# The T1 operands' norm, difference and split go tile by tile and ahead of the fourth product

## The chip, the cores and the metric

The kernel runs on one core of a Trainium2 chip. The metric is the device time of one execution in microseconds. Beside the runs there is one execution taken by the hardware profiler; its rows give times from the first instruction on. TensorE's instructions stand under PE (matmul) and PEld (weight load), VectorE's under DVE, ScalarE's under ACT, GpSimd's under POOL, and the queue that issues most transfers under SP.

## The reference

One encoder layer for two sequences of 512 tokens (s0, the prompt, and s1, the sample), width 1024, in float32. What matters here are its last two parts:

```
h = h + concat(y_pool, y_att) @ w_o
u2 = rms_norm(h, ln2)
h = h + (silu(u2 @ w_gate) * (u2 @ w_up)) @ w_down        # 1024 -> 2816 -> 1024
gate = sigmoid(rms_norm(h, ple_norm) @ w_ple_gate)        # 1024 -> 1024
return h + gate * (p @ w_ple_proj)
```

`rms_norm` divides each token's row by its root mean square and multiplies by a gain per feature.

## The kernel before, in words

Activations lie with features on the 128 partitions and the 512 tokens of a sequence along the free dimension; a feature tile is 128x512. Every float32 product is made of three matmuls (`mm3`, L155 to L157): each operand is split into a high part (ScalarE, L128) and a low part, the rest (VectorE or GpSimd, L131), and high x high (L155), high x low of the activations (L156) and low x high (L157) are summed in PSUM.

Gate, up, down and the embeddings' gate are multiplied in the Winograd form of Strassen's scheme: the two sequences and the two halves of the features make a 2x2 block matrix of activations, two 128-wide column blocks of a weight and the two halves of its rows make the other, and seven products take the place of eight. The activations' operands are B11 and B21 (the first and the second half of s0's normed features) and B22 (the second half of s1's), as they are, and T1 = x12 - x11, T2 = x22 - T1, T4 = x21 - T2, T3 = x22 - x12, where x11 and x21 are s0's halves and x12 and x22 are s1's. Each operand is four tiles of 128 features, so each product is 4 x 3 = 12 matmuls.

`seven` (L679) is a generator that issues the seven products of one pair of weight columns: B11 into a bank a, B21 into a bank c, then it yields; then T1 into b, T2 on top of a, T4 into d, T3 on top of a, B22 on top of b. `got` (L711) copies a, b, and d out of PSUM on ScalarE (L714, into a buffer of the tag F) and adds on DVE (L717). `values4` and its callers make the outputs of them. Weights come from `stationary` (L629): a raw load of 512 KB (tag R, two buffers, L141, SP queue), totals of weight blocks on DVE (L641, tag G, four buffers), splits into eight buffers of tag W; `fill` asks for the next one whenever a product has taken one.

Four pairs are started ahead: their first two products need only s0, and while they run, DVE prepares what s1 gives. `normed_first` (L737) makes B11 and B21, `normed_rest` (L745) the five other operands. A norm is one DVE instruction a tile (`normed`, L727), which reads h, the gain and rb, a PSUM bank of tag g that holds 1/rms for all partitions; rb is made by `norm_rows`. Banks of c, b and d come alternately from the tags pt and g, two banks each; the fourth a is in the tag y. `difference` (L624, instruction L626) makes T1 in an F buffer and T3 in a G buffer; T2 (L756) and T4 (L759) are written over T1.

The order of instructions on an engine isn't the order of the program text: a planner simulates the program and gives each engine, whenever it is free, the earliest instruction of the text that is ready then and has its buffer. The order is fixed at build time; on the chip an engine waits for semaphores. In gate/up (L876 on) a pair is one f for `w_gate` or `w_up`, products of gate and up are multiplied and their seven operands are stored to HBM for the down stage (`spill`, L842), which loads them through the POOL queue (L917). At the embeddings' gate (L971 on) there are four pairs in all, which are started together and finished in order; their outputs go to HBM through the SP queue (L968).

Of the kernel before, what the change touches and what calls it, by code (L numbers as in the profile page):

```python
# [82 lines left out]
G_LN1, G_LN2, G_PLE, G_QA, G_KVA, G_PS, G_QN, G_KN, G_END = 0, 8, 16, 24, 27, 29, 33, 34, 35  # L83
# [3 lines left out]
def hybrid_layer(ctx: ExitStack, tc: tile.TileContext, a: dict, out: bass.AP):  # L87
# [10 lines left out]
    def sbuf(s, tag, shape, dt):  # L98
        return pool.tile([P] + shape, dt, tag=tag, name=nm(s), bufs=BUFS[tag])

    def At(s, tag="A", dt=F32R):
        return sbuf(s, tag, [2, T], dt)
# [9 lines left out]
    def eng(name, i=0):  # L112

        return nc.gpsimd if TURNS[name][i % len(TURNS[name])] == "p" else nc.vector

    def Ps(s, tag=None):
        if tag is None:
            tag = ALL_BANKS[turn[0] * 3 % 8]
            turn[0] += 1
        return psum.tile([P, T], F32, tag=tag, name=nm(s), bufs=PSUM_BUFS[tag])  # L120
# [4 lines left out]
    def split(hi, lo, src, hi_eng="act", lo_eng=nc.vector):  # L125

        if hi_eng == "act":
            nc.scalar.activation(hi, src, AF.Copy)  # L128
        else:
            nc.vector.tensor_copy(hi, src)  # L130
        lo_eng.tensor_tensor(lo, src, hi.bitcast(F32), op=ALU.subtract)  # L131
# [21 lines left out]
    def mm3(ps, lhs, rhs, first, last, more=False):  # L153

        nc.tensor.matmul(ps, lhs[0], rhs[0], start=first, stop=False, skip_group_check=more)  # L155
        nc.tensor.matmul(ps, lhs[0], rhs[1], start=False, stop=False, skip_group_check=more)  # L156
        nc.tensor.matmul(ps, lhs[1], rhs[0], start=False, stop=last, skip_group_check=more)  # L157

    def act(t, sl=slice(0, T), rows=P):
        return t[:rows, 0, sl], t[:rows, 1, sl]  # L160
# [27 lines left out]
    def norm_columns(sq):  # L188

        ps = Ps("st", "g")  # L190
        for t in range(NT):
            nc.tensor.matmul(ps[:, t:t + 1], sq[:, tok(t)], ones[:, 0:1], start=True, stop=True)
        base = col("base")
        nc.vector.tensor_scalar(base[:, :NT], ps[:, :NT], 1.0 / D, EPS, op0=ALU.mult, op1=ALU.add)
        return rsqrt(base[:, :NT], NT, "r")

    def norm_rows(r, copy=True):

        diag = Ft("diag")
        for t in range(NT):  # L200
            nc.vector.tensor_scalar(diag[:, tok(t)], ident, r[:, t:t + 1], None, op0=ALU.mult)
        ps = Ps("rb", "g")
        nc.tensor.matmul(ps, ones, diag, start=True, stop=True)
        if not copy:
            return ps
        rb = Ft("rb")
        nc.scalar.activation(rb, ps, AF.Copy)
        return rb
# [410 lines left out]
    def pieces(u, name, src, tag, lo):  # L619
        d = At("u", tag)  # L620
        split(d[:, 0, :], d[:, 1, :], src, lo_eng=lo)
        u.setdefault(name, []).append(d)

    def difference(x, y, e, tag="F"):  # L624
        d = sbuf("td", tag, [T], F32)
        e.tensor_tensor(d, x, y, op=ALU.subtract)  # L626
        return d
# [44 lines left out]
    def fill():  # L672
        while len(made) < AHEAD:
            w = next(stream, None)
            if w is None:
                return
            made.append(w)

    def seven(u, n, got, a_tag=None, tags=(None,)):  # L679


        def product(ps, b, first):
            w = made.pop(0)
            for j in range(n):
                mm3(ps, (w[:, 0, j * P:(j + 1) * P], w[:, 1, j * P:(j + 1) * P]), act(b[j]), first and j == 0, j == n - 1,
                    not first)
            fill()
            return ps

        def bank(name):  # L690
            t = tags[turn[0] % len(tags)]
            if t is not None:
                turn[0] += 1
            return Ps(name, t)

        a = product(Ps("a", a_tag), u["B11"], True)
        got(0, a)
        got(1, product(bank("c"), u["B21"], True))
        yield
        b = product(bank("b"), u["T1"], True)  # L700
        got(2, b)
        got(3, product(a, u["T2"], False))
        got(4, product(bank("d"), u["T4"], True))
        got(5, product(a, u["T3"], False))
        got(6, product(b, u["B22"], False))
# [19 lines left out]
    def normed(q, gc, k, rb, dst, i):  # L725
        if eng("norm", i) is nc.vector:
            nc.vector.scalar_tensor_tensor(dst, q.h[k], gcol(gc + k), rb[0], op0=ALU.mult, op1=ALU.mult)  # L727
        else:
            nc.scalar.activation(dst, q.h[k], AF.Copy, scale=gcol(gc + k))
            if len(rb) == 1:  # L730
                rb.append(Ft("rb"))
                nc.scalar.activation(rb[1], rb[0], AF.Copy)
            nc.gpsimd.tensor_tensor(dst, dst, rb[1], op=ALU.mult)

    HALF = KD // 2
# [7 lines left out]
                pieces(u, name, s0.u[j][:, i, :], TAGS[name], eng(f"n{i}", j))  # L743

    def normed_rest(gc, u, rb):  # L745
        x = [At("x1", "A", F32) for _ in range(HALF)]
        x12, x22 = ([v[:, i, :] for v in x] for i in range(2))
        for j in range(HALF):
            normed(s1, gc, j, rb, x12[j], 2)
        t = []  # L750
        for j in range(HALF):
            t.append(difference(x12[j], s0.u[j][:, 0, :], eng("tdif", 0)))
            pieces(u, "T1", t[j], TAGS["T1"], eng("n2", j))
        for j in range(HALF):
            normed(s1, gc, j + HALF, rb, x22[j], 3)
            eng("tdif", 1).tensor_tensor(t[j], x22[j], t[j], op=ALU.subtract)  # L756
            pieces(u, "T2", t[j], TAGS["T2"], eng("n3", j))
        for j in range(HALF):
            eng("tdif", 2).tensor_tensor(t[j], s0.u[j][:, 1, :], t[j], op=ALU.subtract)  # L759
            pieces(u, "T4", t[j], TAGS["T4"], eng("n6", j))  # L760
        t3 = []
        for j in range(HALF):
            t3.append(difference(x22[j], x12[j], eng("t3", j), "G"))
            pieces(u, "B22", x22[j], TAGS["B22"], eng("n4", j))
        for j in range(HALF):
            pieces(u, "T3", t3[j], TAGS["T3"], eng("n5", j))

    def run(*gens):
        for g in gens:
            for _ in g:  # L770
                pass
# [46 lines left out]
    u = {}  # L818
# [4 lines left out]
    PRO = len(HB)  # L823
# [10 lines left out]
    rb = [norm_rows(norm_columns(s1.sq), False)]  # L834
# [13 lines left out]
    def gate_up(f):  # L848
        gate = {}

        def gated(i, q, x):
            nc.scalar.activation(x, x, AF.Silu)
            gate[i, q] = x

        hid = {}

        def up(i, q, x):
            nc.vector.tensor_tensor(x, x, gate[i, q], op=ALU.mult)
            hid[i, q] = x
            j = f // 2  # L860
            if (i, q) != (0, s1):
                spill({(0, s0): "B11", (1, s0): "B21", (1, s1): "B22"}[i, q], j, x, eng("hlo", 0))
                return
            x11, x21, x22 = hid[0, s0], hid[1, s0], hid[1, s1]
            t1 = difference(x, x11, eng("hadd", 0))
            spill("T1", j, t1, eng("hlo", 1))
            t3 = difference(x22, x, eng("hadd", 1))
            spill("T3", j, t3, eng("hlo", 2))
            nc.vector.tensor_tensor(t1, x22, t1, op=ALU.subtract)
            spill("T2", j, t1, eng("hlo", 3))  # L870
            nc.vector.tensor_tensor(t1, x21, t1, op=ALU.subtract)
            spill("T4", j, t1, eng("hlo", 4))
        return values4(gated), values4(up)

    pairs = [gate_up(f) for f in range(0, NF, 2)]
    started = []  # L876
    for i in range(PRO):
        g = seven(u, HALF, pairs[i // 2][i % 2], HB[i], OB)
        next(g)
        started.append(g)  # L880
    normed_rest(G_LN2, u, rb)
    for q in seqs:
        for j in range(HALF):
            nc.sync.dma_start(hsave[q.s][j], q.hp[j])
# [24 lines left out]
    for n in DOWN:  # L909
        f1 = f0 + 2 * n  # L910
        u = {}
# [6 lines left out]
        for m in range(0, KD, 2):  # L918
# [6 lines left out]
            def got(i, ps, m=m):  # L925
                for h, k in ((s0.h[m], 0), (s0.h[m], 1), (s1.h[m + 1], 2), (s1.h[m], 3), (s0.h[m + 1], 4),
                             (s0.h[m + 1], 5), (s1.h[m + 1], 5), (s1.h[m], 6)):
                    if i == k:
                        nc.vector.tensor_tensor(h, h, ps, op=ALU.add)  # L929
# [25 lines left out]
    u = {}  # L955
    rb = [[norm_rows(c, False)] for c in r]
# [13 lines left out]

    pairs = [ple(m) for m in range(0, KD, 2)]  # L971
    started = [seven(u, HALF, got, HB[i], OB) for i, got in enumerate(pairs)]
    for g in started:
        next(g)
    normed_rest(G_PLE, u, rb[1])
    run(*started)


# [94 lines left out]
```

## Time and profile before

| what | value |
|---|---|
| runs | 1200.99, 1203.9, 1204.89 us; median 1203.9 |
| the profiled execution | 1204.31 us |
| its span, first to last instruction | 1202.5 us |
| granted TensorE clock, mean over the span | 0.976 |
| gate/up begins, with the start of the first products, until | about 424 to 861 us |
| embeddings' gate | about 1110 to 1199 us |

The time of an execution is a little longer than its span. A row of a timeline gives the start, the duration, the engine, the line, the operation with out<-in (buffer numbers left out), how many instructions are merged, and in brackets how long the engine had been idle and what released it. Matmuls are pipelined, so the durations of neighbours overlap: 0.39 us long, they start 0.23 us apart at full clock.

### The profile page before, as it was taken

How to read it: one execution, taken by the hardware profiler on the slowest of the kernel's cores; microseconds unless marked ns; L12 is line 12 of the kernel's file. 1: busy time of each engine (PE TensorE's matmuls, PEld its weight loads, DVE VectorE, ACT ScalarE, POOL GpSimd, SP SyncE). 2: the span in 40 equal slices, each digit the busy share in tenths (PEclk: the TensorE clock that was granted, in tenths of full speed). 3: DMA queues.
4: the chain of work that ended last, by engine and by line, in shares of the span. 5: the costliest groups of instructions: out<-in, count | busy, mean ns of one | idle time of the engine just before them, and what ended most of it. 6: DMA issues, size and time to landing. Idle time of an engine off the chain costs nothing.

```text
span 1202.5 us, 15165 instructions
## 1 busy us (share of the span) xinstructions
PE 1137.3 (95%) x5232; PEld 938.9 (78%) x5232; DVE 926.4 (77%) x1738; ACT 592.2 (49%) x1135; POOL 241.3 (20%) x276
## 2 busy tenths in 40 slices
PE   8999989996999989999999999999969999999897
PEld 8898767784888867888888888888748888887675
DVE  7377889999774789987767877677658768884798
ACT  7154468777663535654545454455312222444553
POOL 3533553746240220000000000001312122001200
PEclk9899989998999999999999999999979999999999
DMA  6211100102233431554335442456978395626036
GB/s 215 69 56 55 38 1 1 53 15 74 88 108 121 140 105 53 196 189 175 122 124 192 152 177 100 150 193 236 404 289 321 120 352 183 250 66 210 26 122 220
DMA packets 53646, 173.28 MB, mean 144 GB/s; under 512 B 6208, under 2 KB 6976, under 8 KB 53568
## 3 DMA queue, kind: packets, MB, share of 16 engines
q1 hardware_dynamic: 41328, 127.73, 31.3%
q0 software_dynamic: 12240, 44.57, 9.6%
q8 instruction: 41, 0.67, 0.2%
q14 instruction: 37, 0.30, 0.1%
HBM read 119.33 MB, written 52.95 MB: 143 GB/s over the span
## 4 chain that ended last, share of the span: by engine, by line
PE 74%; DVE 14%; issue 5%; DMA 3%; POOL 2%; ACT 2%; SPq 0%; POOLq 0%; DVEq 0%; ACTq 0%
PE a L156 7%; PE a L157 7%; PE a L155 7%; PE b L155 5%; PE b L156 5%; PE b L157 5%; PE d L157 2%; PE d L156 2%; PE d L155 2%; PE o L155 2%; PE o L156 2%; PE o L157 2%; PE c L155 2%; PE c L157 2%; PE c L156 2%
## 5 line engine op out<-in xcount | busy, mean ns | idle before, releaser
L155 PE MATMUL a<-u,w 128*128 128x512 f32 x444 | 171.6, 392 | 10.0 <-ACT w L128 9.4
L156 PE MATMUL a<-u,w 128*128 128x512 f32 x444 | 174.0, 392 | 0.6 <-DVE u L131 0.3
L157 PE MATMUL a<-u,w 128*128 128x512 f32 x444 | 171.8, 391 | 1.0 <-DVE w L131 1.0
L128 ACT ACTIVATE w<-s 128x512 fp32r<-128x512 f32 (+2 forms) x168 | 97.2, 579 | 150.2 <-PE b L157 49.5
L128 ACT ACTIVATE w<-raw 128x512 fp32r<-128x512 f32 (+2 forms) x126 | 71.0, 577 | 172.2 <-PE a L157 98.1
L155 PE MATMUL b<-u,w 128*128 128x512 f32 x296 | 116.3, 394 | 6.8 <-DVE h L929 6.1
L131 DVE TENSOR_TENSOR w<-s,w 128x512 fp32r<-128x512 f32 (+2 forms) x168 | 104.2, 622 | 23.3 <-ACT w L128 22.6
L156 PE MATMUL b<-u,w 128*128 128x512 f32 x296 | 115.8, 392 | 3.7 <-DVE u L131 3.7
L157 PE MATMUL b<-u,w 128*128 128x512 f32 x296 | 116.0, 392 | 1.1 <-DVE w L131 1.1
L155 PEld LDWEIGHTS a<-u,w 128*128 128x128 f32 x444 | 83.8, 189 | 29.5 <-ACT w L128 10.6
L131 DVE TENSOR_TENSOR w<-raw,w 128x512 fp32r<-128x512 f32 (+2 forms) x126 | 78.4, 635 | 30.7 <-ACT w L128 30.7
L156 PEld LDWEIGHTS a<-u,w 128*128 128x128 f32 x444 | 83.8, 189 | 19.5 <-DVE u L131 1.5
L157 PEld LDWEIGHTS a<-u,w 128*128 128x128 f32 x444 | 83.8, 189 | 19.2 <-DVE w L131 1.9
L917 POOL DMA_DIRECT2D u<-opT4p x11 | 6.2, 563 | 414.8 <-DVE s L641 363.0
L155 PEld LDWEIGHTS b<-u,w 128*128 128x128 f32 x296 | 56.1, 189 | 20.2 <-DVE h L929 6.5
L156 PEld LDWEIGHTS b<-u,w 128*128 128x128 f32 x296 | 55.8, 189 | 16.6 <-DVE u L131 5.1
L157 PEld LDWEIGHTS b<-u,w 128*128 128x128 f32 x296 | 55.8, 189 | 13.4 <-DVE w L131 1.9
L155 PE MATMUL c<-u,w 128*128 128x512 f32 x148 | 58.9, 401 | 5.2 <-DVE x L727 5.2
L157 PE MATMUL c<-u,w 128*128 128x512 f32 x148 | 58.9, 398 | 0.0
L156 PE MATMUL c<-u,w 128*128 128x512 f32 x148 | 58.8, 397 | 0.0
L131 POOL TENSOR_TENSOR wl<-raw,wh 128x1024 fp32r<-128x1024 f32 (+4 forms) x24 | 50.2, 2095 | 37.1 <-ACT wh L128 32.8
L157 PE MATMUL d<-u,w 128*128 128x512 f32 x148 | 57.6, 389 | 0.0
(243 smaller groups left out, 2858.3 us busy)
## 6 DMA issues: line engine op xcount, KB each, us to landing
raw<-in_w_gate SPq DMA_DIRECT2D x24, 512.0 KB, 4.2
raw<-in_w_up SPq DMA_DIRECT2D x24, 512.0 KB, 3.6
raw<-in_w_down SPq DMA_DIRECT2D x24, 384.0 KB, 3.8
raw<-in_w_o SPq DMA_DIRECT2D x16, 512.0 KB, 3.6
raw<-in_w_pg SPq DMA_DIRECT2D x12, 512.0 KB, 3.7
opB11p<-st SPq DMA_DIRECT2D x11, 512.0 KB, 2.6
opB21p<-st SPq DMA_DIRECT2D x11, 512.0 KB, 3.7
opT1p<-st SPq DMA_DIRECT2D x11, 512.0 KB, 4.3
```

The lines of the kernel that those rows point to most:

```text
L128: nc.scalar.activation(hi, src, AF.Copy)
L131: lo_eng.tensor_tensor(lo, src, hi.bitcast(F32), op=ALU.subtract)
L155: nc.tensor.matmul(ps, lhs[0], rhs[0], start=first, stop=False, skip_group_check=more)
L156: nc.tensor.matmul(ps, lhs[0], rhs[1], start=False, stop=False, skip_group_check=more)
L157: nc.tensor.matmul(ps, lhs[1], rhs[0], start=False, stop=last, skip_group_check=more)
L917: nc.gpsimd.dma_start(d.bitcast(F32), spilled[k][f0 // 2 + j])
```

## The change

In `normed_rest` the norm of a T1 tile, the difference and the split stand in one loop over the four tiles, where the four norms had a loop of their own. Behind that loop the function yields, so that it can be run in two parts. At gate/up the first part stands ahead of the fourth pair's first two products in the program, where all of it stood behind them; the rest (T2, T4, T3, B22) stays behind them. At the embeddings' gate it is the same. No instruction is added or removed.

```diff
     def normed_rest(gc, u, rb):
+
         x = [At("x1", "A", F32) for _ in range(HALF)]
         x12, x22 = ([v[:, i, :] for v in x] for i in range(2))
+        t = []
         for j in range(HALF):
             normed(s1, gc, j, rb, x12[j], 2)
-        t = []
-        for j in range(HALF):
             t.append(difference(x12[j], s0.u[j][:, 0, :], eng("tdif", 0)))
             pieces(u, "T1", t[j], TAGS["T1"], eng("n2", j))
+        yield
         for j in range(HALF):
             normed(s1, gc, j + HALF, rb, x22[j], 3)
...
     pairs = [gate_up(f) for f in range(0, NF, 2)]
     started = []
+    rest = normed_rest(G_LN2, u, rb)
     for i in range(PRO):
+        if i == PRO - 1:
+            next(rest)
         g = seven(u, HALF, pairs[i // 2][i % 2], HB[i], OB)
         next(g)
         started.append(g)
-    normed_rest(G_LN2, u, rb)
+    run(rest)
...
     pairs = [ple(m) for m in range(0, KD, 2)]
     started = [seven(u, HALF, got, HB[i], OB) for i, got in enumerate(pairs)]
-    for g in started:
+    rest = normed_rest(G_PLE, u, rb[1])
+    for i, g in enumerate(started):
+        if i == PRO - 1:
+            next(rest)
         next(g)
-    normed_rest(G_PLE, u, rb[1])
+    run(rest)
     run(*started)
```

## Rows read from the trace of the kernel before

**Rows 1.** The page's busy times: engine, us (share of span), instructions.

```profile
PE 1137.3 (95%) x5232; PEld 938.9 (78%) x5232; DVE 926.4 (77%) x1738; ACT 592.2 (49%) x1135; POOL 241.3 (20%) x276
```

**Rows 2.** Windows: stretch, its length, busy us by engine (instructions), PE's clock, DMA share.

```profile
440.00:450.00 10.00, 4.76 (x20) 3.62 (x19) 8.68 (x14) 2.15 (x4) 0.00 (x0) 0.91 0.04 14
450.00:460.00 10.00, 8.39 (x27) 6.31 (x26) 10.00 (x18) 2.82 (x5) 0.00 (x0) 0.75 0.01 2
...
1130.00:1140.00 10.00, 6.80 (x27) 4.62 (x27) 10.00 (x18) 6.66 (x13) 0.00 (x0) 1.00 0.09 36
```

**Rows 3.** Timeline of PE at gate/up: start, us, instruction [idle before <-releaser].

```profile
449.32 0.77 PE L155 MATMUL c<-u,w 128*128 128x512 f32 x1 [5.24 <-DVE x L727]
...
454.15 0.63 PE L157 MATMUL c<-u,w 128*128 128x512 f32 x1
...
457.04 0.50 PE L156 MATMUL b<-u,w 128*128 128x512 f32 x1 [1.61 <-DVE u L131]
...
463.06 0.50 PE L156 MATMUL a<-u,w 128*128 128x512 f32 x1 [0.29 <-DVE u L131]
...
485.81 0.39 PE L157 MATMUL b<-u,w 128*128 128x512 f32 x1
```

**Rows 4.** The tile rb: who waited for its instructions (us, times).

```profile
  PE c L155: 5.2, 1
```

**Rows 5.** Timeline of DVE at gate/up.

```profile
441.29 0.69 DVE L641 TENSOR_TENSOR s<-raw 128x512 f32<-128x512 f32 x1 [2.02 <-DMA raw<-in_w_up]
442.01 0.69 DVE L641 TENSOR_TENSOR s<-s,raw 128x512 f32<-128x512 f32 x1
...
443.82 5.35 DVE L727 SCALAR_TENSOR_TENSOR x<-h,gain,rb 128x512 f32<-128x512 f32 x8
449.09 0.68 DVE L717 TENSOR_TENSOR x<-x,c 128x512 f32<-128x512 f32 x1
...
450.89 2.49 DVE L626 TENSOR_TENSOR td<-x,x 128x512 f32<-128x512 f32 x4
...
457.51 1.89 DVE L131 TENSOR_TENSOR u<-td,u 128x512 fp32r<-128x512 f32 x3
...
474.98 0.68 DVE L641 TENSOR_TENSOR s<-raw,s 128x512 f32<-128x512 f32 x1
...
480.09 0.69 DVE L641 TENSOR_TENSOR s<-raw 128x512 f32<-128x512 f32 x1 [1.43 <-DMA raw<-in_w_gate]
...
483.10 0.68 DVE L131 TENSOR_TENSOR w<-s,w 128x512 fp32r<-128x512 f32 x1
```

**Rows 6.** Timeline of the SP queue at gate/up.

```profile
475.12 0.90 SPq L141 DMA_DIRECT2D raw<-in_w_gate  x2
```

**Rows 7.** Timeline of PE at the embeddings' gate.

```profile
1134.03 0.50 PE L156 MATMUL b<-u,w 128*128 128x512 f32 x1 [1.32 <-DVE u L131]
...
1137.63 0.50 PE L156 MATMUL b<-u,w 128*128 128x512 f32 x1 [0.80 <-DVE u L131]
...
1139.44 0.50 PE L157 MATMUL b<-u,w 128*128 128x512 f32 x1 [1.07 <-DVE w L131]
...
1166.45 0.40 PE L157 MATMUL b<-u,w 128*128 128x512 f32 x1
```

**Rows 8.** Timeline of DVE at the embeddings' gate.

```profile
1129.07 0.69 DVE L131 TENSOR_TENSOR w<-s,w 128x512 fp32r<-128x512 f32 x1 [1.18 <-ACT w L128]
...
1162.40 0.69 DVE L641 TENSOR_TENSOR s<-raw 128x512 f32<-128x512 f32 x1 [1.11 <-DMA raw<-in_w_pg]
...
1165.62 0.68 DVE L131 TENSOR_TENSOR w<-s,w 128x512 fp32r<-128x512 f32 x1
```

**Rows 9.** Timeline of ACT at the embeddings' gate: the copies of a.

```profile
1128.95 0.58 ACT L714 ACTIVATE x<-a 128x512 f32<-128x512 f32 x1
...
1130.93 0.58 ACT L714 ACTIVATE x<-a 128x512 f32<-128x512 f32 x1
```

## The prediction

> **What bounds the kernel now.** I read the page's busy line first: TensorE (PE) is busy for 95% of the span and VectorE (DVE) for 77% [rows 1]. So the kernel is a TensorE kernel on average, and a change of order can only pay in the stretches in which TensorE starves. Next I read the windows by stage. In the two stretches around the change the reader sees the roles exchanged: from 440 to 460 us DVE is busy nearly throughout, PE runs 20 and 27 matmuls in ten microseconds where 44 fit, and the granted clock is 0.91 and 0.75; from 1130 to 1140 DVE is full again and PE runs 27, at full clock [rows 2].
>
> Then the timeline of PE, which shows the places. At gate/up it waits 5.24 us before the c product of the fourth started pair, runs that product at 0.63 us a matmul instead of 0.39 (the low one of its two clock levels, after the wait), waits 1.61 us for the first T1 products (b) and 0.29 for T2 (accumulated in a) [rows 3], and then no more up to the next pairs. The view of the tile rb names what the first wait is for: the norms that read rb out of the PSUM bank that this product takes over [rows 4]. At the embeddings' gate there are three small waits, 1.32, 0.80 and 1.07 us, the first two for T1's low parts, the third for a weight [rows 7].
>
> Last the timeline of DVE, since DVE is what PE waits for. At gate/up the eight norms run in one piece, 5.35 us from 443.82, then the add of c (449.09), and the four T1 differences only at 450.89, though the program writes them ahead of the second four norms [rows 5]. I infer why: the order on each engine is planned, and buffers of one tag are given out in the program's order; a difference takes an F buffer, and so does the copy of the fourth a, which the old program asks for first. From 443.82 to the weight total that ends at 475.7 no row of DVE shows idle time. After it the sync queue can fetch the next raw weights (475.12), they let DVE begin at 480.09 after 1.43 us idle, and the low part of the first new weight stands at 483.10 to 483.78 [rows 5, 6]. PE needs it at 485.81 [rows 3].
>
> **The change part by part.** It adds and removes no instruction and no DMA. It moves twelve DVE instructions (four norms, four differences, four low parts) and four of ScalarE (high parts) ahead of the fourth pair's two products and its copy, at two places.
>
> *The norms at gate/up.* Four norms of T1 now stand first, at 5.35 / 8 = 0.66 us each [rows 5]; differences and low parts cost 2.49 / 4 = 0.62. The norms of the second half come behind them. The add at 449.09 belongs to the c that uses the other bank of rb's pair. In the old order eight norms fit ahead of it; now about eight of the twelve moved instructions do: 4 x 0.66 + 4 x 0.62 = 5.1 us. So I expect the fourth c to take the bank that this add frees, at about the time at which it starts now. The 5.24 us stay, within the bounds of 0 (its bank is free at once) and 5.24 plus some microseconds (below). I take it as unmoved, since the row that holds it, an add behind eight instructions, looks the same afterwards.
>
> *What follows it.* The other four of the twelve and the low parts of T1 are done by about 453, before the fourth c ends (454.8), where now they end at 459.4 [rows 3, 5]. So the 1.61 us go, and the T2 operands, which now have DVE's turn from 453 instead of 460, take the 0.29 with them: 1.90 us. Is it kept? The third pair needs the weight at 485.81 and it stands at 483.78, so 2.03 us of room: 1.90 just fits. More would be held there, unless DVE's stretch up to 475.7 gets shorter; two multiplications of the next pairs that were slipped in early might move behind it, at 0.62 us each. So at most 2.03 + 1.24 = 3.3 us at this place, and at least 0 when the room is eaten.
>
> *A price of tile by tile.* A norm is followed by the difference that reads it. Two dependent DVE instructions in this trace start 0.72 us apart (441.29 and 442.01), four independent ones 0.60 ((2.49 - 0.68) / 3) [rows 5]. Eight such neighbours would be 1.0 us, none 0; the planner can put another tile's instruction between, so I take 0.3 us of DVE time, inside the room above. [...]
>
> *The embeddings' gate.* All sixteen norms are long done here; what moves is the differences and parts. They waited for the copy of the fourth a (1130.93 on ScalarE) and now wait for that of the third (1128.95), 1.98 us earlier [rows 9]. DVE is idle for 1.18 us ahead of 1129.07 [rows 8], full from 1130 to 1140 [rows 2], and its next wait of any length is the 1.11 us for raw weights at 1162.40 [rows 8]. PE's three waits of 3.19 us [rows 7] could go, but the next pair's weight (low part ending at 1166.3) is used at 1166.45 [rows 7, 8]: only 0.15 us of room. So what counts is how much earlier DVE gets through, that is, how much of the idle time the moved instructions fill: 0 to 1.18 us. I take 0.7.
>
> The sum: 1.90 + 0.7 = 2.6 us. The profiled execution took 1204.31 us, 1.8 more than its span and 0.4 more than the median of 1203.9; so 1201.7 for it and 1201.3 for the median. A measurement of this kernel can't tell less than about 0.3%, 3.6 us, from no change, so the likeliest case lies inside that.
>
> **The rivals.**
>
> *The first wait goes too.* If the planner gives the fourth c the bank that is free at 443.9, PE saves 5.24 us of waiting and runs twelve matmuls 0.2 us faster, 2.4 us. For it: the second half's norms, which held the bank, are later now, so another bank is the natural one. Against it: PE would run into T1 and T2 operands that DVE can't give before it has done 24 instructions, and into the weight; 3.3 us at most are kept. With the embeddings' waits gone as well (3.19 us, if DVE's 1.18 and 1.11 us of idle time are used and the weight comes with it) that is 3.3 + 3.2 = 6.5 us: 1197.4 us. [...]
>
> *Hidden anyway.* The raw weights of the third pair come no earlier and are used a little later for the 0.3 us above, or T3's last operand, which DVE makes just before, holds PE instead. Then PE waits at 480 for what it no longer waits for at 455. For it: DVE has no idle time from 443.82 to 475.7, and no work is taken off it. Against it: the 2.03 us of room. It gives 1203.5 us.
>
> *Slower: the add of c slides behind the norms.* If the fourth c still takes rb's bank, or if DVE is planned to run through T1 and on into the second half's norms before the add, the product waits for 12 + 4 or more instructions instead of 8: 8 x 0.64 = 5.1 us later, of which the 1.90 us of waits that follow are absorbed: 3.2 us lost, and 5.8 if T2's four differences go ahead as well. It decides as soon as three more instructions than now (1.9 us) stand ahead of the add. For it: with the F buffers open, nothing stops DVE from running on. Against it: the add comes earlier in the program than all of these, and is taken when ready. It gives 1203.9 + 3.2 to 5.8, less the embeddings' 0.7: 1206.4 to 1209.
>
> **How the numbers follow.** The likeliest case 0.42 (its own range 1199.5 to 1203; 0.13 of it, with DVE's idle stretches filled more than I count, lies beyond 3.6 us), the first wait gone 0.25, hidden 0.15, slower 0.18. Faster by over 0.3%: 0.25 + 0.13 = 0.38. Slower by over 0.3%: most of the slower case and no other, 0.17. The rest, 0.45, is within 0.3%. The range runs from 1196.0, somewhat below the case with the first wait gone, to 1207.0, inside the slower case; that leaves 0.1 on either side, for the order of everything behind the change is planned anew, the change of stage at 850 us included.
>
> **What the profile would show.** Right: T1 differences among the first four norms at gate/up, the fourth c starting near 449 us, no wait of b for low parts, PE at the third pair's T1 about 2 us earlier, and the raw load of about 475 unmoved. At the embeddings' gate T1 differences ahead of 1130 us, less idle time on DVE before them. It would be wrong if the fourth c starts without a wait and PE keeps more than 3.3 us (then the weights were not the limit), if it starts after 451 us (then DVE ran ahead of the add), or if the difference arises between 850 and 900 us, which the argument does not reach.

## The result and the profile after

The changed kernel takes 1213.16 us in the median (1212.67 to 1213.81, four runs), the kernel before 1202.69 us in the four runs beside it: a ratio of 1.0088, 95% interval 1.0068 to 1.0108. That is slower by 10.5 us, outside the range of the prediction. The profiled execution took 1213.49 us, with a span of 1211.7 us and a mean granted clock of 0.974; both kernels run the same instructions.

The page's busy times after hardly differ from [rows 1]: 9 us of span were added, and no engine's busy time grew by more than PE's 4.1 us.

```profile
PE 1141.4 (94%) x5232; PEld 942.1 (78%) x5232; DVE 928.5 (77%) x1738; ACT 591.8 (49%) x1135; POOL 241.6 (20%) x276
```

First, gate/up. The windows of after from 440 to 460, then the timelines of PE, of DVE and of the SP queue there:

```profile
440.00:450.00 10.00, 7.89 (x28) 5.55 (x27) 8.33 (x14) 3.05 (x6) 0.00 (x0) 0.89 0.05 22
450.00:460.00 10.00, 7.71 (x26) 5.07 (x24) 10.00 (x18) 3.53 (x6) 0.00 (x0) 0.84 0.01 2
```

```profile
446.28 0.50 PE L155 MATMUL b<-u,w 128*128 128x512 f32 x1 [1.88 <-ACT u L128]
447.00 0.50 PE L156 MATMUL b<-u,w 128*128 128x512 f32 x1 [0.22 <-DVE u L131]
448.24 0.76 PE L155 MATMUL c<-u,w 128*128 128x512 f32 x1
...
456.97 0.51 PE L156 MATMUL b<-u,w 128*128 128x512 f32 x1 [2.29 <-DVE u L131]
461.78 0.79 PE L156 MATMUL b<-u,w 128*128 128x512 f32 x1 [1.73 <-DVE u L131]
```

```profile
444.10 0.74 DVE L727 SCALAR_TENSOR_TENSOR x<-h,gain,rb 128x512 f32<-128x512 f32 x1
444.87 0.69 DVE L626 TENSOR_TENSOR td<-x,x 128x512 f32<-128x512 f32 x1
...
447.47 0.68 DVE L717 TENSOR_TENSOR x<-x,c 128x512 f32<-128x512 f32 x1
...
451.74 3.38 DVE L727 SCALAR_TENSOR_TENSOR x<-h,gain,rb 128x512 f32<-128x512 f32 x5
...
455.63 0.69 DVE L626 TENSOR_TENSOR td<-x,x 128x512 f32<-128x512 f32 x1
...
461.04 0.69 DVE L131 TENSOR_TENSOR u<-td,u 128x512 fp32r<-128x512 f32 x1
```

```profile
476.24 0.89 SPq L141 DMA_DIRECT2D raw<-in_w_gate  x2
```

PE runs 28 and 26 matmuls in the two windows, at a clock of 0.89 and 0.84, where [rows 2] have 20 and 27. T1 differences stand among the norms now. PE begins a T1 product at 446.28, ahead of the fourth c, and so the 5.24 us of [rows 3] in front of that c are gone. But the last norm of T1 comes with the four of the second half in one piece (451.74), the last difference only at 455.63, and the last low part ends at 461.73 (459.40 in [rows 5]); PE waits there for 2.29 and 1.73 us. The waits in these rows come to 6.12 us, where [rows 3] have 7.14. The raw weights are asked for at 476.24, 1.12 us later than in [rows 6]. What becomes of it is read at the first norm of the embeddings' gate: it starts at 1108.55, and at 1108.45 before. So the whole loss in these two profiles arises behind that point.

The embeddings' gate: DVE before, then DVE after.

```profile
1108.45 10.62 DVE L727 SCALAR_TENSOR_TENSOR x<-h,gain,rb 128x512 f32<-128x512 f32 x16 [9.07 <-PE rb L203]
1120.72 0.69 DVE L131 TENSOR_TENSOR w<-s,w 128x512 fp32r<-128x512 f32 x1 [1.64 <-ACT w L128]
...
1157.37 0.68 DVE L641 TENSOR_TENSOR s<-raw,s 128x512 f32<-128x512 f32 x1
...
1193.73 1.28 DVE L717 TENSOR_TENSOR x<-x,a 128x512 f32<-128x512 f32 x2 [1.57 <-issue]
```

```profile
1108.55 6.01 DVE L727 SCALAR_TENSOR_TENSOR x<-h,gain,rb 128x512 f32<-128x512 f32 x9 [8.82 <-PE rb L203]
1120.82 0.69 DVE L131 TENSOR_TENSOR w<-s,w 128x512 fp32r<-128x512 f32 x1 [6.25 <-ACT w L128]
...
1127.31 0.69 DVE L626 TENSOR_TENSOR td<-x,x 128x512 f32<-128x512 f32 x1
...
1129.79 0.74 DVE L727 SCALAR_TENSOR_TENSOR x<-h,gain,rb 128x512 f32<-128x512 f32 x1
...
1137.78 2.71 DVE L727 SCALAR_TENSOR_TENSOR x<-h,gain,rb 128x512 f32<-128x512 f32 x4
1140.41 0.68 DVE L131 TENSOR_TENSOR u<-td,u 128x512 fp32r<-128x512 f32 x1
1141.01 0.68 DVE L626 TENSOR_TENSOR td<-x,x 128x512 f32<-128x512 f32 x1
...
1161.48 0.68 DVE L641 TENSOR_TENSOR s<-raw,s 128x512 f32<-128x512 f32 x1
...
1184.68 0.69 DVE L970 TENSOR_TENSOR x<-x,e 128x512 f32<-128x512 f32 x1 [2.47 <-DMA e<-emb]
1185.29 0.69 DVE L971 TENSOR_TENSOR x<-x,h 128x512 f32<-128x512 f32 x1
1185.89 0.69 DVE L641 TENSOR_TENSOR s<-s,raw 128x512 f32<-128x512 f32 x1
...
1200.93 0.69 DVE L717 TENSOR_TENSOR x<-x,b 128x512 f32<-128x512 f32 x1 [2.32 <-issue]
1203.65 1.28 DVE L717 TENSOR_TENSOR x<-x,a 128x512 f32<-128x512 f32 x2 [2.03 <-PE a L157]
```

Before, sixteen norms run in one piece; after, nine. DVE then stands idle for 6.25 us, not 1.64, and the other seven norms follow from 1129.79 to 1140.49, in the stretch in which DVE has no idle time at all. The last T1 difference starts at 1141.01. The last weight total of the second of the four pairs (L641; the raw weights of the third are asked for behind it) starts 4.1 us later (1161.48 for 1157.37), which is the 4.6 us of norms less 0.6 us that the early difference takes out of the 1.18 us of [rows 8]. PE shows the consequence; its timeline after:

```profile
1141.14 0.79 PE L156 MATMUL b<-u,w 128*128 128x512 f32 x1 [3.45 <-DVE u L131]
1141.74 0.63 PE L157 MATMUL b<-u,w 128*128 128x512 f32 x1
1142.16 0.63 PE L156 MATMUL b<-u,w 128*128 128x512 f32 x1
...
1146.56 0.51 PE L156 MATMUL b<-u,w 128*128 128x512 f32 x1 [1.96 <-DVE u L131]
...
1187.35 0.50 PE L155 MATMUL a<-u,w 128*128 128x512 f32 x1 [2.26 <-ACT w L128]
...
1189.03 0.63 PE L155 MATMUL b<-u,w 128*128 128x512 f32 x1
1189.46 0.63 PE L156 MATMUL b<-u,w 128*128 128x512 f32 x1
```

In place of the waits of [rows 7] it waits 3.45 and 1.96 us. The second half of the loss is at the end: DVE stands for 2.47 us before a load of `e`, with the last pair's total (1185.89) queued behind it, and PE waits 2.26 us for the weight made from that. The wait for `e` is half of that second half. DVE is busy for 38.5 us behind the second pair's last total in both kernels, and idle for 3.54 us there before and 8.55 after. Most of the 8.55 are the 2.47 us for `e`, 1.39 us for PE at 1165.35, and 2.32 and 2.03 us at the very end, where before has 1.57. The SP queue's waits from 1150 us on say why the load is late; first before, then after (us in total, times, longest):

```profile
SPq L963 <- DMA out_y<-x: 3.3, 3, 2.5
```

```profile
SPq L967 <- DMA out_y<-x: 10.2, 4, 4.1
```

A load of `e` takes an F buffer, and that comes free when a store of the output has ended.

### The profile page after: what moved, and what is told of

Its sections match the earlier page's. It is cut to its first block, busy times and chain, and to the rows that moved or that the text cites. A ratio compares the mean times of both kernels' runs of the same rounds, so it can differ in the third digit from the quotient of the medians.

```text
span 1211.7 us, 15158 instructions
## 1 busy us (share of the span) xinstructions
PE 1141.4 (94%) x5232; PEld 942.1 (78%) x5232; DVE 928.5 (77%) x1738; ACT 591.8 (49%) x1135; POOL 241.6 (20%) x276
## 4 chain that ended last, share of the span: by engine, by line
PE 73%; DVE 14%; issue 5%; DMA 4%; POOL 2%; ACT 2%; SPq 0%; DVEq 0%; POOLq 0%; ACTq 0%
PE a L156 7%; PE a L157 7%; PE a L155 7%; PE b L157 5%; PE b L156 5%; PE b L155 5%; PE d L155 2%; PE d L156 2%; PE d L157 2%; PE o L155 2%; PE o L156 2%; PE o L157 2%; PE c L155 2%; PE c L157 2%; PE c L156 2%
## 5 line engine op out<-in xcount | busy, mean ns | idle before, releaser
L156 PE MATMUL b<-u,w 128*128 128x512 f32 x296 | 118.5, 400 | 10.1 <-DVE u L131 10.1
L155 PE MATMUL b<-u,w 128*128 128x512 f32 x296 | 117.8, 401 | 8.2 <-DVE h L933 4.8
L157 PE MATMUL b<-u,w 128*128 128x512 f32 x296 | 117.9, 398 | 0.5 <-DVE w L131 0.5
L156 PEld LDWEIGHTS b<-u,w 128*128 128x128 f32 x296 | 57.0, 192 | 24.3 <-DVE u L131 12.8
L155 PEld LDWEIGHTS b<-u,w 128*128 128x128 f32 x296 | 56.8, 192 | 22.9 <-DVE h L933 5.2
L157 PEld LDWEIGHTS b<-u,w 128*128 128x128 f32 x296 | 57.0, 193 | 12.8 <-DVE w L131 1.2
```

## The experiments

The theory after this reading, "buffer order": the planner gives out the buffers of one tag in the order in which the program first writes them (the four x buffers are declared ahead of the loop in both kernels). The norm of tile j+1 needs a new x buffer of tag A, and in the tile-by-tile loop that stands behind the split buffer `u` of tile j, tag A too; the split waits for the difference, the difference for an F buffer behind the copies of a. So norms are held at the embeddings' gate. Rivals: the place ahead of the fourth product; the tile-by-tile sequence as such (dependent neighbours); gate/up.

**The two places apart (e1, e2).** Each restores the old text of `normed_rest` and its old place at the other place.

```diff
     for i, g in enumerate(started):          # embeddings' gate, e1
-        if i == PRO - 1:
-            next(rest)
         next(g)
```

> The change at gate/up alone; at the embeddings' gate everything as before. Theory (buffer order: in the tile by tile loop the norm of the next tile takes an A buffer that is given out only after the split of the tile before has got its own, so at the embeddings' gate seven of the sixteen norms leave VectorE's idle time, 7 x 0.66 = 4.6 us, and land where VectorE is full): gate/up changes nearly nothing, since there is no idle time there to lose: 1201.5 to 1204. Rival 1 (the T1 instructions ahead of the fourth product are in the way of what the running products need, at both places): about half of the loss here, 1206 to 1209. Rival 2 (the change of stage at 850 us is planned anew and costs): 1206 and more, with the difference between 850 and 900 us.

> The change at the embeddings' gate alone; gate/up as before. Theory (buffer order): the whole loss, 1211.5 to 1214, and only 9 of the 16 norms ahead of 1115 us. Rival 1 (in the way, at both places): 1206 to 1209. Rival 2 (change of stage): 1202 to 1204.

Gate/up alone: 1201.78 us, ratio 0.9986 (0.997 to 1.0003). The embeddings' gate alone: 1213.28 us, ratio 1.0079 (1.0049 to 1.0109). The loss belongs to the embeddings' gate; gate/up gives what can't be told from nothing.

**Norms in a loop of their own, and buffers asked for early (e3, e4).** Two ways to bring the sixteen norms back, both with the part ahead of the fourth product kept.

```diff
+        for j in range(HALF):                # e3
             normed(s1, gc, j, rb, x12[j], 2)
+        for j in range(HALF):
             t.append(difference(...))
...
+        for v in x:                          # e4
+            nc.gpsimd.memset(v[:, 0, 0:1], 0.0)
         for j in range(HALF):
             normed(s1, gc, j, rb, x12[j], 2)
```

> The change in both places, but the four norms in a loop of their own ahead of the differences, as before the change; the position ahead of the fourth product stays. Theory (buffer order): the four x buffers are asked for ahead of the split buffers, all sixteen norms run early again, the loss goes: 1199 to 1204. Rival 1 (the position is what costs): 1209 to 1214, as with the change.

> The changed kernel with one addition: GpSimd writes one column of each of the four x buffers ahead of the tile by tile loop, so that the buffers are given out in the order of a loop of norms, while program order of norm, difference and split stays tile by tile. Theory (buffer order): within 1 us of the run with the norms first, 1199 to 1204. Rival (it is the tile by tile order of the instructions itself, the dependent neighbours on VectorE): 1211 to 1214.

1204.46 us (ratio 1.0014, 0.9998 to 1.003), just above what was expected, and 1204.56 us (1.0008, 0.9991 to 1.0025). The second keeps the tile-by-tile text and only fixes the order in which four buffers are given out; the row of DVE in it is that of before again:

```profile
1107.17 10.62 DVE L727 SCALAR_TENSOR_TENSOR x<-h,gain,rb 128x512 f32<-128x512 f32 x16 [9.72 <-PE rb L203]
```

The two kernels agree within 0.1 us, and their traces have all instructions of PE, ACT and DVE in the same order from start to end. So the order of the buffers alone decides here in which order norms and differences run, and the sequence in the program text, with the buffers' order fixed, changes nothing. That the part stands further ahead gained nothing, though.

**The loop behind, and DVE work alone (e5 to e7).** The next kernel has the tile-by-tile loop in the old place at both places (the two `next(rest)` are taken out of the changed kernel). Two others leave the kernel before as it is and add seven DVE instructions, early and late in the full stretch.

```diff
             t.append(difference(x12[j], ...))
+            for _ in range((1, 1, 1, 4)[j] if gc == G_PLE else 0):    # e6
+                nc.vector.tensor_tensor(t[j], t[j], t[j], op=ALU.max)
...
             eng("tdif", 2).tensor_tensor(t[j], ...)                   # T4
+            for _ in range((1, 2, 2, 2)[j] if gc == G_PLE else 0):    # e7
+                nc.vector.tensor_tensor(t[j], t[j], t[j], op=ALU.max)
```

> The tile-by-tile loop of norm, difference and split, in the old place behind the fourth pair's first products, at both places: nothing is moved ahead. Buffer order: a norm's buffer stands behind the split of the tile before in the order in which the tag A is given out, so the norms at the embeddings' gate are held as in the changed kernel: nine in one piece at about 1108 us, DVE idle for about 6 us before 1121, and a time of 1211 to 1216 us. Since the differences now also wait for the copy of the fourth a instead of the third, it may be up to 2 us above the changed kernel. The place ahead as cause: 16 norms in one piece and about the time of the kernel before, 1201 to 1205 us.

> The kernel before with seven more DVE instructions at the embeddings' gate, a maximum of each T1 difference with itself (which changes no value), one behind each of the first three differences and four behind the last: about as many and as long as the norms that the changed kernel leaves to this stretch, and at about the same point of the order. All sixteen norms run early as before. Full stretch: the loss is DVE's time in a stretch in which DVE sets the pace, so seven instructions of 0.60 to 0.66 us cost at least 4.2 us, and if the other 4.5 us of the loss follow from the lateness too (weights later, lower clock, the end of the last pairs), the time is near the changed kernel's: 1207 to 1214 us. Rival, waits on buffers: the loss comes from the wait of the norms for buffers and not from their DVE time; then PE has cover for these instructions and the time stays within 3 us of the kernel before, 1201 to 1206 us.

> The same seven instructions, later: behind the differences of T4 (one, two, two and two), of which the product comes after those of T1 and T2; T1 and T2 are not delayed. If the loss goes by DVE's total in the full stretch (up to about 1157 us no DVE idle time), the place doesn't matter: the same time as with the seven behind T1's differences, within 2 us. If it goes by the lateness of T1 (PE starves, its clock falls, and what is lost there isn't made up), this one is near the kernel before: 1202 to 1206 us.

The loop behind: 1210.94 us, ratio 1.0066 (1.0043 to 1.0089), a hair below what the theory said; the place is not the cause. Seven instructions ahead of T1's parts: 1210.85 us, 1.0062 (1.0038 to 1.0086); behind: 1210.69 us, 1.0073 (1.0047 to 1.0099). So seven instructions of 0.6 us in this stretch, with the loops and the buffers as before, cost 7 to 9 us at either place. The two traces don't lose it at the same point, though: the table below has the loss of the first ahead of the second pair's last total and that of the second behind it.

**The other way (e8, e9).** If DVE's time in the full stretch sets the end, taking work out of it must gain. Gate/up stays as changed; at the embeddings' gate the norms have their own loop and the part that makes T1 stands ahead of the third (e8) or second (e9) of the four pairs:

```diff
     for i, g in enumerate(started):
+        if i == 2:        # e9: if i == 1
+            next(rest)
         next(g)
```

> Gate/up as in the changed kernel; at the embeddings' gate the four norms of T1 stand in a loop of their own again, and the part that makes T1 stands further ahead, before the third of the four pairs begins instead of before the fourth. Then T1's differences and low parts take their buffers ahead of the copies of the third and the fourth a. Full stretch: it cuts the other way too. The T1 differences can run in DVE's idle time before 1130 us, eight instructions of 0.60 us at most, four for the differences alone; PE's three waits for T1 and a weight (3.19 us) go, and each instruction that leaves the full stretch is worth about what one more cost, 0.6 to 1.0 us: 1195 to 1200 us, 2 to 7 us below the kernel with gate/up alone changed. Rival: the raw weights or the last pair's own work set the end, and only more work hurts while less work gives nothing: 1200.5 to 1204 us.

> The same with that part one pair further ahead, before the second of the four pairs begins: T1's buffers stand ahead of the copies of the second, third and fourth a. DVE's idle time before 1125 us is open to all eight T1 instructions. Full stretch: the same gain or up to 2 us more than with the part ahead of the third pair, 1193 to 1200 us. Rival: the copies of the a banks, now behind, hold PE or the weights at the start, and nothing is gained: 1200.5 to 1206 us.

1199.32 us (ratio 0.9964, 0.9951 to 0.9977) and 1197.81 us (0.9955, 0.994 to 0.9969): both faster than before, and the interval of the second lies below that of gate/up alone. DVE in the second:

```profile
1104.49 10.62 DVE L727 SCALAR_TENSOR_TENSOR x<-h,gain,rb 128x512 f32<-128x512 f32 x16 [8.90 <-PE rb L203]
1115.02 3.37 DVE L626 TENSOR_TENSOR td<-x,x 128x512 f32<-128x512 f32 x4
1118.32 1.28 DVE L131 TENSOR_TENSOR w<-s,w 128x512 fp32r<-128x512 f32 x2
1119.52 2.48 DVE L131 TENSOR_TENSOR u<-td,u 128x512 fp32r<-128x512 f32 x4
```

No idle time is left behind the norms, and PE's two waits up to 1142 us are 0.41 and 0.20 us.

**A smaller dose (e10).** As the kernel with four buffers asked for, but only three (`for v in x[:3]`).

> The changed kernel with three of the four buffers of T1's norms asked for ahead of the loop (GpSimd sets one column of each to zero). The planned order has eleven norms in one piece at the embeddings' gate, where there are nine with none asked for and sixteen with all four. Full stretch: five norms stay in the stretch in which DVE sets the pace, at 1.0 to 1.35 us each: 1207 to 1211 us, between the kernel with four asked for (1204.6) and the changed one (1213.2). Rival, one held norm is enough, since the first T1 product waits for its last tile: as the changed kernel, 1212 to 1215 us.

1202.84 us, ratio 1.0001 (0.9986 to 1.0015): a miss on both sides, five held norms cost next to nothing. Its DVE rows:

```profile
1104.17 7.33 DVE L727 SCALAR_TENSOR_TENSOR x<-h,gain,rb 128x512 f32<-128x512 f32 x11 [9.55 <-PE rb L203]
1116.39 0.69 DVE L131 TENSOR_TENSOR w<-s,w 128x512 fp32r<-128x512 f32 x1 [4.89 <-ACT w L128]
...
1122.88 1.89 DVE L626 TENSOR_TENSOR td<-x,x 128x512 f32<-128x512 f32 x3
...
1126.49 1.40 DVE L727 SCALAR_TENSOR_TENSOR x<-h,gain,rb 128x512 f32<-128x512 f32 x2
```

With three norms ready three differences run at 1122.88, in time in which DVE was idle before. So held norms are the wrong unit. The unit is DVE's idle time, and this makes one table of all runs. Worked out from each profile's DVE timeline: the norms in the first piece; the idle time from its start to the last total of the second pair's weight; the length of that stretch, which is DVE's busy time plus its idle time; and the length from there to DVE's last instruction.

| run | ratio | norms | idle, us | to the total, us | from there, us |
|---|---|---|---|---|---|
| before | 1 | 16 | 5.98 | 48.92 | 42.17 |
| after | 1.0088 | 9 | 9.99 | 52.93 | 47.06 |
| gate/up alone | 0.9986 | 16 | 5.95 | 48.89 | 42.04 |
| embeddings' gate alone | 1.0079 | 9 | 9.98 | 52.92 | 44.93 |
| norms first | 1.0014 | 16 | 4.76 | 47.61 | 47.11 |
| four buffers asked for | 1.0008 | 16 | 4.78 | 47.63 | 46.55 |
| loop behind | 1.0066 | 9 | 10.88 | 53.90 | 43.37 |
| seven more, early | 1.0062 | 16 | 6.65 | 53.89 | 42.94 |
| seven more, late | 1.0073 | 16 | 5.98 | 49.51 | 52.35 |
| ahead of the third pair | 0.9964 | 16 | 0 | 43.92 | 43.68 |
| ahead of the second pair | 0.9955 | 16 | 0 | 43.91 | 43.68 |
| three buffers asked for | 1.0001 | 11 | 8.05 | 50.89 | 42.16 |

In before and after 42.9 us of the stretch are busy in both, and the 4.0 us between them are idle time. Three buffers give 2.07 us more of it than before and 1.97 us more length. The time did not follow there: it is that of before, and 1.8 us more at the interval's upper end. The last column is a second thing, the order planned for the end. It is 42.0 to 42.2 us in three of the runs in which DVE never waits for `e` there and 43.37 in the fourth (the loop behind), 47.06 with the wait of 2.47 us shown above, and 52.35 with three (2.33, 1.29 and 2.98 us). With norms first and with four buffers asked for it is another wait: PE stands 2.97 and 3.28 us before a b bank until ScalarE has copied it, and what the stretch to the total won is lost there.

Each row of the table is one execution, and the ratio is of medians. The profiled execution with norms first was the slowest of its twelve (1211.02 us, median 1204.46), and that of seven more, late, lies 3.5 us above its median. Much of such a spread arises ahead of this stage: with norms first it begins at 1111.55 us, and with four buffers asked for, the same order of instructions, at 1107.17. Within the stage runs with one order agree: 47.11 and 46.55 us for these two in the last column, 42.17 and 42.04 us for before and gate/up alone, which have one order of DVE and PE here. After and the embeddings' gate alone have one order on DVE up to the total (52.93 and 52.92 us) and two behind it (47.06 and 44.93).

So the two columns together account for the times only roughly: the idle time up to the total tells the changed kernels from those with sixteen norms early, but the times of norms first, four buffers, three buffers and seven late can't be read from it alone.

**Without `e` (e11, e12).** Both kernels without the loads of `e`; the output multiplies by h in its place.

```diff
-            e = Ft("e")
-            nc.sync.dma_start(e, emb[m + i, :, q.s, :])
...
-            oe.tensor_tensor(x, x, e, op=ALU.mult)
+            oe.tensor_tensor(x, x, q.h[m + i], op=ALU.mult)
```

> The kernel before without the loads of the embeddings' projection (e): the output multiplies by h in its place, so the product with the projection is left out of the result, and 16 loads of 256 KB on the sync queue with it. This is the base for the changed kernel without the same loads. Either theory: at or somewhat below the kernel before, 1195 to 1204 us, since at its end few instructions wait for e.

> The changed kernel without the loads of e, the output multiplied by h in its place, as in the run beside it. The first part of the loss (DVE's idle time of 4 us more up to the last total of the third pair's weights) has nothing to do with e and must stay. The second part (about 5 us from that total to the end): if it comes from DVE standing before a late e (2.47 us at 1184.68), with the last pair's weight behind it, it goes, and the difference to the kernel before without e is 3 to 6 us. Rival: it comes from PE's starving and the clock that falls with it, or from the lateness of the T1 products as such, and then it stays: a difference of 7.5 to 11 us.

1207.2 us (ratio 1.0036, 1.0022 to 1.005) and 1208.31 us (1.0039, 1.0025 to 1.0053). The base itself became slower by 3.5 us, against the expectation: multiplications that no longer wait for `e` are planned into the full stretch (busy 45.9 us there, not 42.9). The first part stayed, 9.41 us idle for 5.40 up to the second pair's last total (which the expectation calls the third's). The second part is gone and more: 40.65 us from the total to the end, and 43.44 in the base. So it doesn't follow from PE's waits and its clock in the T1 products, which are there in this run too (waits of 1.91, 3.27 and 1.82 us, with matmuls of 0.63 us from 1133.85, 1140.75 and 1147.36 on). But the difference of 1.1 us is below both expectations, 3 to 6 and 7.5 to 11 us: the first part did not come through to the end either (in the base DVE waits 7.63 us for PE at 1195.97). With a base that moved it is no clean subtraction, and the wait for `e` as the cause of the second part is read from the trace, not shown by these two runs.

## Why the prediction was wrong, step by step

*What bounds the kernel* was read rightly: PE starves for what DVE makes. At the embeddings' gate a longer way of DVE to the second pair's last total went with a longer time in most runs, with the exceptions named under the table.

*The step that failed* is the first sentence on the embeddings' gate: "All sixteen norms are long done here; what moves is the differences and parts." It took the place of the norms in the trace as given, while the change had put them behind the splits in the order in which tag A is given out. The prediction had that rule in hand, and used it for the F buffers of differences and copies alone; that `x1` and T1's parts share the tag A stands in the code. What the runs showed in its place: nine norms run early and seven run in the full stretch, and the buffers' order alone brings the sixteen back (ratio 1.0008 for 1.0088). So the term of 0.7 us gained was 4.0 us lost by the last total of the second pair, and 4.9 us more at the end. The range had no case for it, and it held a forecast whose sign was wrong.

*The first wait at gate/up.* "The 5.24 us stay" failed too: the c took the bank that the add frees, as said, but that add stood behind five of the moved instructions, not eight (447.47), and PE had a T1 product to run meanwhile.

*What follows it.* The waits of 1.61 and 0.29 us did not go; 2.29 and 1.73 us stand in their place, since the fourth norm of T1 was late here too (451.74). The statement that DVE has no idle time there and that no work is taken off it, made for the rival "hidden anyway", fits what came: the change at gate/up alone gave 0.14%, with an interval that holds no change.

*The price of tile by tile*, 0.3 us, was too high: in the changed kernel one T1 difference alone stands right behind its norm, at gate/up, 0.77 us after its start (444.10 and 444.87) where independent norms stand 0.66 apart [rows 5]. That is 0.11 us in all, since the planner put other instructions between the rest.

*The slower rival* had the right sign and a quarter to a half of the size (1206.4 to 1209), by luck: it named the add of c at gate/up, which came earlier and not later. *The first wait goes too*: the wait went, but not by the rival's condition, since the c still took the bank that the add frees, and no gain came of it that the runs can tell from none.

**What stays open.** Three of the seven held norms (x12) lack a buffer. The four of the second half (x22) use the other halves of the same buffers, and still came only behind the fourth norm of T1, even where three buffers had been asked for; why the planner held them wasn't tried. The second part of the loss was read from the trace as a chain (output store, F buffer, load of `e`, DVE, weight), and it is gone without `e`; why the order planned for the end meets that wait in some versions and not in others stays open, as does the share of the loss that is this wait's.

## What to carry to other kernels

Where an engine is full in one stretch and idle just before it, ask of each moved or re-ordered instruction whether it now runs in the idle time and whether it still will: list, for each buffer tag, who takes its buffers in the order of the program, before and after. Where buffers are given out in the program's order, a loop that interleaves a producer with a consumer that is held by something else holds the producer, too, if both take buffers of one tag. And a stage is best compared from its first fixed instruction to a late fixed one on the full engine, as busy plus idle time: that showed here where 4.0 us of the loss arose, which waits and instruction counts did not; what comes behind that point has to be read by itself.

## What the runs showed of the hardware

TensorE's clock fell after waits of 1.96 to 3.45 us. In the window from 1140 to 1150 us of after the mean granted clock is 0.70, with the waits of 3.45 and 1.96 us, and behind the first matmuls start 0.42 to 0.43 us apart instead of 0.23; in the single microseconds from 1141 to 1144 and from 1148 to 1150 the granted clock is 0.50. Before, with waits of 1.32, 0.80 and 1.07 us in the ten microseconds ahead [rows 7], the clock stayed at 1.00:

```profile
1140.00:1150.00 10.00, 9.32 (x40) 7.14 (x39) 10.00 (x17) 6.84 (x12) 0.00 (x0) 1.00 0.02 6
```

```profile
1140.00:1150.00 10.00, 6.90 (x18) 5.10 (x19) 10.00 (x17) 5.34 (x10) 0.00 (x0) 0.70 0.00 0
```

The first is before, the second after. The single wait of 2.26 us that ends at 1187.35 was also followed by matmuls that start 0.42 to 0.43 us apart, from 1189.03 to 1191.59, with a granted clock of 0.50 from 1189 to 1191. The 0.63 us a matmul of the prediction's c product go with the same figure: in before the single microseconds from 449 to 455 have a granted clock of 0.50, those from 456 to 466 one of 1.00.

A VectorE difference took longer beside GpSimd. In the version ahead of the second pair the first of the four differences at 1115.02 took 1.561 us and the others 0.68; GpSimd's low parts ran until 1116.03. The instructions of that line (duration in ns, least, median, most):

```profile
L626 DVE TENSOR_TENSOR td<-x,x x4: 676/678/1561, 1115.0 to 1117.7; 128x512 f32<-128x512 f32 x4
```

```profile
1105.97 10.06 POOL L131 TENSOR_TENSOR u<-x,u 128x512 fp32r<-128x512 f32 x8 [11.30 <-ACT u L128]
```

That difference ended 0.55 us behind the end of GpSimd's row. The version ahead of the third pair has the same: a first difference of 1.571 us that ended 0.55 us behind GpSimd's low parts (1116.80). The norms beside the same GpSimd work, which read one of their two tiles from PSUM, didn't take longer: sixteen in 10.62 us, 0.66 us each, as the eight of [rows 5].
